# Two hybrid blocks on one core: the first block's gates, projection up and mixture laid out by channel, and the second attention's outputs turned ahead of the last fill

## The chip, the cores and the metric

The kernel runs on one core of a Trainium2 chip. The metric is the device time of one execution in microseconds (us); lower is better. The core has TensorE (PE; its weight loads are shown as PEld), VectorE (DVE), ScalarE (ACT), GpSimd (POOL) and the DMA queue engine SyncE (SP), each with an instruction queue of its own.

## The reference, cut to what matters

512 tokens of width 1024 pass through two blocks, all in float32. The first block mixes two attentions and then has a mixture of experts; the second has a recurrent branch and an attention of its own. The change touches the mixer of the first block only:

```
h = rms_norm(x, norm_mix_g)                       # 512 x 1024
(f_q, f_k, f_v, f_f, n_q, ..., g_a, g_b) = split_cols(h @ w_in)   # g_a, g_b: 1024 columns each
out_a = from_heads(fox_attention(...)) @ w_fox_up     # 512 x 512 @ 512 x 1024
out_b = from_heads(nsa_attention(...)) @ w_nsa_up     # 512 x 512 @ 512 x 1024
mix = sigmoid(g_a) * out_a + sigmoid(g_b) * out_b
x = x + mix @ w_out
x = x + hierarchical_moe(rms_norm(x, norm_ffn_g), ...)
```

The kernel takes a sigmoid as 0.5 * (1 + tanh(z / 2)), and leaves the factor 0.5 to the very end of the mixture.

## The kernel before, in words

**Products.** Float32 operands are kept as a high and a low half (`split`: ACT copies the high half, DVE subtracts), and each product is three matmuls (`mm3`). `linear_steps` makes a product of all tokens with some columns of a weight: tokens stand (128 at a time), weights move (256 or 512 columns), and the result lies with tokens on the partitions. It returns two lists of steps with a nominal cost each: loads (a DMA on SP, and the two halves of the weights by ACT and by DVE or POOL in turns, `weight_piece`), and products (one slice of 128 of the inner dimension each; the last one of a token tile calls `emit`, which empties the bank). Results go through the PSUM banks of tag "mm", of which there are two. A buffer is handed on when all who use it are done.

**Normalisation.** `hh` and `hl` are the halves of x * gain, turned (channels on partitions). The factor 1/rms of each token, `c.r`, with `c.rh` = `c.r` / 2, is applied when a bank is emptied; with tokens on the partitions it is a column of 128 scalars, and ACT takes it as the scale of its instruction.

**The mixer, `first_mixer`.** PE runs in the order in which the code is written (`manual_schedule`); on the other engines a planner orders the instructions by its own cost model. After a start-up, `A.run` goes through 24 attention jobs (8 heads of the first attention, 16 of the second) in 72 units: scores of one unit, transposes of the unit before, values of the one before that. Between them `fill.pull` takes steps from a long list (`Fill`) until their nominal costs reach the given time. The list holds, in this order, the input projections (q, k, v, kw, nq), small steps ("start"), the gates of the second attention (`gate`, four jobs of 256 channels, g0 to g512 and g), the turning of the first attention's outputs (`turn`), and four times 256 channels of the first attention's gate and projection up (`up`: a0, u0, ...). In `gate` ACT takes Tanh of the bank and SP stores it to `gd`. In `up` ACT takes Tanh (`gated`), and when the projection up of the same channels is done, DVE makes (1 + tanh) * product (`emit`), stored to `md` by ACT's queue. `gd` and `md` lie in DRAM with tokens as rows. `second` and `trig` prepare vectors for the second block; their tiles `small` and `cs` have the tag t, of which there are two buffers.

What is left of the list at the end of the attention run is done by `fill.until(None)`. Then `token_T` turns the second attention's outputs `ob` (four token tiles: four transposes on PE into an mm bank, a copy by ACT, four subtractions by DVE), and `merge` does the rest for each half of the channels: it loads `gd` and `md`, multiplies the outputs with `w_nsa_up` (512 columns moving), and per token tile DVE makes (1 + gate) * product and adds the other half of the mixture; four transposes on PE turn it, and ACT and DVE split it into `mh` and `ml`. These stand in the output projection, `out_proj` (in `route`), which begins right behind, token tile by token tile with eight products each. Then come the router and the experts, whose weights are streamed.

The lines that matter: `linear_steps` L128 to L148, `tanh_to_dram` L150, `token_T` L169, `merge` L181, `r_row` L248, `gate` L682, `turn` L688, `up` L694, the jobs L710 to L733, the run and what follows L771 to L782, `trig` L1921.

Of the kernel before, what the change touches and what calls it, by code (L numbers as in the profile page):

```python
# [10 lines left out]
FT = mybir.dt.float32  # L11
FR = mybir.dt.float32r
# [3 lines left out]
AF = mybir.ActivationFunctionType  # L16
OP = mybir.AluOpType
# [4 lines left out]
S = 512  # L22
D = 1024
NT = 4
# [16 lines left out]
class Ctx:  # L41
# [105 lines left out]
        return ([(max(1, g * n // 512), lambda k0=k0: load(k0)) for k0 in range(0, K, 128 * g)],  # L147
                [(3 * n / 2400, lambda i=i, k=k: product(i, k)) for i in range(NT) for k in range(K // 128)])  # L148

    def tanh_to_dram(self, pool, dst):  # L150

        def emit(i, ps):
            sg = pool.tile([128, 512], FT, name="sg", bufs=2)
            n = ps.shape[1]
            self.nc.scalar.activation(sg[:, :n], ps, AF.Tanh, scale=self.rh[:, i:i + 1])
            self.nc.sync.dma_start(dst(i), sg[:, :n])
        return emit

    def silu2_to_dram(self, pool, dst, scale=lambda i: 0.5):

# [84 lines left out]
        self.rh = self.sm.tile([128, NT], FT, name="rxh", bufs=1)  # L245
        nc.vector.tensor_scalar(self.rh, self.r, 0.5, None, op0=OP.mult)

    def r_row(self, t):  # L248

        n = t.shape[0]  # L250
        ps = self.bank("pt", [128, S])
        for i in range(NT):
            self.nc.tensor.matmul(ps[:n, 128 * i:128 * i + 128], self.r[:, i:i + 1].to_broadcast([128, n]), self.ident,
                                  start=True, stop=True)
        self.nc.scalar.activation(t, ps[:n], AF.Copy)
# [279 lines left out]
def first_mixer(c, I, at, hh, hl):  # L535

    nc, tc = c.nc, c.tc
    w_in = I["w_in"][0]
# [5 lines left out]
    def big(name, tag):  # L544
        return at.tile([128, NT, 512], FT, name=name, tag=tag, bufs=1)
# [13 lines left out]
    x = [big("x", t).rearrange("p (a i) n -> p a (i n)", a=2) for t in ("t0", "t1", "zk", "b2")]  # L559
    x, xgs, scr = [x[i // 2][:, i % 2] for i in range(4)], [x[3][:, i] for i in range(2)], x[2][:, 1]  # L560
# [11 lines left out]
    pt = c.bank("x", [128, S])  # L572
# [70 lines left out]
    N = Nsa(c, at)  # L643
# [12 lines left out]
    def fox(h):  # L656
        def scale():
            if h % 2 == 0:
                two["q"] = A.scaled(z["zq"][:, :, 64 * h:64 * h + 128].rearrange("p i (a d) -> p i a d", a=2),
                                    fx["q"][:, :, h:h + 2])  # L660
            two["k"] = A.twice(z["zk"][:, :, 64 * h:64 * h + 64], fx["k"][:, :, h:h + 1])

        def queries():
            if h % 2 == 0:
                qs[h:h + 2] = A.queries(two["q"], c.cv["fox_q"])

        def prep():
            k = A.keys(two["k"], c.cv["fox_k"])
            cb = at.tile([128, S], FT, name="cb", bufs=2)
            nc.sync.dma_start(cb, _ap(cumd, h * S, [[0, 128], [1, S]]))  # L670

            return A.passes(qs[h], k), lambda i: cb[:, :128 * (i + 1)], True

        def done(pv, rb, ri):

            nc.vector.scalar_tensor_tensor(z["zq"][:, :, 64 * h:64 * h + 64], pv, fx["v"][2], rb, op0=OP.mult, op1=OP.mult)
        return (scale, queries, prep), lambda: (*fx["v"][:2], h), done


    gd = c.dram.tile([S, D], FT, name="gd")  # L680

    def gate(c0):  # L682
        return c.linear_steps(hh, hl, w_in, 3872 + c0, 256, c.tanh_to_dram(at, lambda i: gd[
            128 * i:128 * i + 128, c0:c0 + 256]))
    md = c.dram.tile([S, D], FT, name="md")
    ot = []

    def turn(i):  # L688
# [4 lines left out]

    def up(c0):  # L694

        m = []

        def gated(i, ps):
            if i % 2 == 0:
                m.append(at.tile([128, 2, 256], FT, name="sg", bufs=2))  # L700
            nc.scalar.activation(m[i // 2][:, i % 2], ps, AF.Tanh, scale=c.rh[:, i:i + 1])

        def emit(i, ps):
            v = m[i // 2][:, i % 2]
            nc.vector.scalar_tensor_tensor(v, v, 1.0, ps, op0=OP.add, op1=OP.mult)
            nc.scalar.dma_start(md[128 * i:128 * i + 128, c0:c0 + 256], v)
        return {f"a{c0}": c.linear_steps(hh, hl, w_in, 2848 + c0, 256, gated),
                f"u{c0}": c.linear_steps(lambda: ot, None, I["w_fox_up"][0], c0, 256, emit)}

    jobs = {}  # L710
    for name, c0 in (("q", 0), ("k", 512), ("v", 1024)):
# [7 lines left out]
    def second():  # L719

        c.vectors([
            ("mu", I["mu_shift_2"], 0), ("w0", I["w0_2"], 0), ("a0", I["a0_2"], 0), ("k_k", I["k_k_2"], 0),
            ("k_a", I["k_a_2"], 0), ("r_k", I["r_k_2"].rearrange("a b -> (a b)"), 0), ("gn_gain", I["gn_gain_2"], 0),
            ("gn_bias", I["gn_bias_2"], 0), ("g_q", I["g_q_2"], 0), ("g_kv", I["g_kv_2"], 0),
        ], "mm")
        late.append(trig(c, I, at))
    jobs |= {f"g{c0}": gate(c0) for c0 in range(0, D - 256, 256)}
    jobs["second"] = ([], [(1.0, second)])
    jobs["g"] = gate(D - 256)
    jobs["trig"] = ([], [(0.5, lambda: late[0]())])  # L730
# [9 lines left out]
    pt = c.bank("pt", [128, NT, 32])  # L740
# [4 lines left out]
    f = at.tile([8, S], FT, name="t", bufs=2)  # L745
# [20 lines left out]
    with tc.manual_schedule(engines={mybir.EngineType.PE}):  # L766
        N.keys(I, A, z["kv"], fill)
        N.values(I, A, z["kv"], fill)
        fill.until("v")
        comp = [f for g in range(2) for f in N.compressed(g)]  # L770
        A.run([fox(h) for h in range(8)] + N.jobs(A, lambda: big("ob", "zk")), fill, lambda u: 2.0 if u <= 22 else 1.62,  # L771
              [(43 + 2 * n, f) for n, f in enumerate(comp)])
        fill.until(None)


    mix = [at.tile([128, 2, D], FT, name="mix", tag=t, bufs=1) for t in ("t0", "t1")]
    mh, ml = (c.hp.tile([128, 8, S], FR, name=n, tag="f16", bufs=2) for n in ("mh", "ml"))
    ot = at.tile([128, 4, S], FR, name="obh", tag="kv", bufs=1), [
        at.tile([128, S], FR, name="obl", tag=t, bufs=n) for t, n in (("p", 3), ("p", 3), ("p", 3), ("cb", 2))]
    c.token_T(N.ob, *ot)  # L780
    c.merge(at, "q", 8, lambda: ot, I["w_nsa_up"][0], gd, md, mix, mh, ml)
    return mh, ml  # L782


# [1136 lines left out]
def trig(c, I, pool):  # L1921

    nc = c.nc
    small = pool.tile([128, 8, NT, 16], FT, name="t", bufs=2)
    pi, pf, inv = small[:, 0, 0, :NT].bitcast(I32), small[:, 1, 0, :NT], small[:, 2, 0]
    nc.sync.dma_start(pi, I["positions_2"].rearrange("a (i p) -> p (a i)", p=128))
    nc.vector.tensor_copy(pf, pi)
    for j in range(16):  # L1930
        nc.gpsimd.memset(inv[:, j:j + 1], float(np.float32(10000.0) ** np.float32(-2.0 * j / 32)))
    sh = [128, NT, 16]
    ang, n = small[:, 3], small[:, 4]
    nc.vector.tensor_mul(ang, pf[:, :, None].to_broadcast(sh), inv[:, None, :].to_broadcast(sh))
    c1 = 6.28125
    c2 = math.floor((2 * math.pi - c1) * 2 ** 20) / 2 ** 20
    c3 = 2 * math.pi - c1 - c2
    cos, sin = small[:, 5], small[:, 6]
    for j, r in ((1, cos), (0, sin)):
        nc.vector.tensor_scalar(n, ang, 1.0 / (2 * math.pi), 0.25 * j, op0=OP.mult, op1=OP.add)  # L1940
        nc.vector.tensor_scalar(n, n, 12582912.0, None, op0=OP.add)
        nc.vector.tensor_scalar(n, n, -12582912.0, None, op0=OP.add)
        nc.vector.scalar_tensor_tensor(r, n, -c1, ang, op0=OP.mult, op1=OP.add)
        nc.vector.scalar_tensor_tensor(r, n, -c2, r, op0=OP.mult, op1=OP.add)
        nc.vector.scalar_tensor_tensor(r, n, -c3, r, op0=OP.mult, op1=OP.add)
        if j:
            nc.vector.tensor_scalar(r, r, math.pi / 2, None, op0=OP.add)
        nc.vector.tensor_scalar(r, r, 3.1415925, -3.1415925, op0=OP.min, op1=OP.max)
    nc.scalar.activation(small[:, 5:7], small[:, 5:7], AF.Sin)
    cs = pool.tile([128, NT, 128], FT, name="t", bufs=2)  # L1950
    nc.gpsimd.memset(cs, 0.0)
    nc.gpsimd.tensor_copy(cs[:, :, 64:80], cos)
    nc.gpsimd.tensor_copy(cs[:, :, 80:96], cos)
    nc.gpsimd.tensor_scalar(cs[:, :, 96:112], sin, -1.0, None, op0=OP.mult)
    nc.gpsimd.tensor_copy(cs[:, :, 112:], sin)
    c.csd = c.dram.tile([128, 2, NT, 16], FT, name="csd")
    nc.sync.dma_start(c.csd, small[:, 5:7])

    def turn():
        pt = c.bank("mm", [128, S])  # L1960
        for i in range(NT):
            nc.tensor.transpose(pt[:, 128 * i:128 * i + 128], cs[:, i], c.ident)
        qs = -1.0 / math.sqrt(96.0)
        csq = pool.tile([128, S], FT, name="sg", bufs=2)
        nc.gpsimd.memset(csq[:64], qs)
        nc.scalar.activation(csq[64:], pt[64:], AF.Copy, scale=qs)
        c.csqd = c.dram.tile([128, S], FT, name="csqd")
        nc.sync.dma_start(c.csqd, csq)
    return turn
# [317 lines left out]
```

## Time and profile before

| | us |
|---|---|
| median of 3 runs | 1434.35 |
| lowest, highest | 1432.84, 1443.26 |
| the profiled execution | 1437.92 |
| its span, first to last instruction | 1436.0 |

The profile is of one execution. Its page gives the busy time of each engine (matmuls are pipelined and their ends are modelled, so a busy PE is not PE at its peak); further views are the busy time by stretch, the list of who waited for whom, groups of instructions, and the timeline, whose times are counted from the first instruction. An L number is a line of the kernel before.

### The profile page before, as it was taken

The page shows a single profiled execution, that of the slowest core. Times are in us where ns is not written, and L with a number is a line of the kernel's source. Part 1 is how long each engine was busy: PE and PEld are TensorE (multiplying, and loading weights), DVE is VectorE, ACT ScalarE, POOL GpSimd, SP SyncE. Part 2 cuts the span into 40 slices and gives each one's busy share as a digit, 9 for nine tenths or more (in the row PEclk, how much of TensorE's full clock was granted, in tenths as well). Part 3 has the DMA queues.
Part 4 walks back from the last instruction along what each step waited for, and adds up shares of the span by engine and source line. Part 5 has one row for each costly group of instructions (what it writes and reads, how often), then busy time and mean ns, then how long its engine had stood idle before and what let it go on. Part 6 is the DMA issues. An engine that isn't in the chain of part 4 may idle for free.

```text
span 1436.0 us, 24621 instructions
## 1 busy us (share of the span) xinstructions
PE 1285.7 (90%) x9232; PEld 1090.5 (76%) x9232; DVE 951.4 (66%) x1907; ACT 753.9 (53%) x1291; POOL 427.3 (30%) x349
## 2 busy tenths in 40 slices
PE   7989777997989896899999997879988998799997
PEld 6889677987889775577777776868976767788875
DVE  5565557556565637799999997646657858525645
ACT  5544445665444322688888874645556664224431
POOL 1333324332332111235555522201123335213211
PEclk9999888999999998899999998989999999799999
DMA  6432222222133388999999986521152234233543
GB/s 195 119 106 76 63 54 61 86 64 66 60 96 115 98 285 328 320 356 364 355 345 359 343 292 209 148 83 48 46 165 74 83 123 123 87 100 115 169 135 118
DMA packets 162445, 230.94 MB, mean 161 GB/s; under 512 B 22426, under 2 KB 99021, under 8 KB 162320
## 3 DMA queue, kind: packets, MB, share of 16 engines
q1 hardware_dynamic: 150912, 205.44, 43.7%
q0 software_dynamic: 6224, 18.62, 4.6%
q10 hardware_dynamic: 5184, 5.25, 1.1%
q8 instruction: 74, 1.21, 0.3%
q14 instruction: 51, 0.42, 0.1%
HBM read 200.89 MB, written 30.36 MB: 161 GB/s over the span
## 4 chain that ended last, share of the span: by engine, by line
PE 37%; DVE 9%; DMA 5%; issue 5%; ACT 4%; POOL 1%; POOLq 0%; DVEq 0%; ACTq 0%; SPq 0%
PE mm L118 8%; PE mm L120 8%; PE mm L119 8%; DMA x2d<-y,slt 2%; PE s L120 2%; PE s L118 2%; PE s L119 2%; DMA raw<-in_w_in 2%; PE s L457 1%; DVE itmp L1766 1%; DVE Ti L1768 1%; DMA raw<-in_w_o 1%; PE pt L484 1%; DMA vmmx<-vmx 1%; POOL wl L112 1%
## 5 line engine op out<-in xcount | busy, mean ns | idle before, releaser
L112 POOL TENSOR_TENSOR wl<-raw,wh 128x512 fp32r<-128x512 f32 x119 | 163.7, 1381 | 462.9 <-ACT wh L109 424.2
L92 DVE TENSOR_TENSOR wl<-rawe,wh 128x1024 fp32r<-128x1024 f32 x192 | 224.8, 1218 | 23.9 <-ACT wh L90 22.9
L109 ACT ACTIVATE wh<-raw 128x512 fp32r<-128x512 f32 x214 | 131.6, 627 | 130.2 <-PE mm L120 57.6
L118 PE MATMUL mm<-wh,hh 128*128 128x256 f32 (+1 forms) x616 | 186.7, 303 | 11.1 <-ACT hh L90 3.5
L90 ACT ACTIVATE wh<-rawe 128x1024 fp32r<-128x1024 f32 x192 | 190.6, 1052 | 2.0 <-PE mm L120 1.8
L119 PE MATMUL mm<-wl,hh 128*128 128x256 f32 (+1 forms) x616 | 179.7, 292 | 0.3 <-DVE wl L112 0.3
L120 PE MATMUL mm<-wh,hl 128*128 128x256 f32 (+1 forms) x616 | 179.8, 292 | 0.1
L118 PEld LDWEIGHTS mm<-wh,hh 128*128 128x128 f32 (+1 forms) x616 | 122.8, 199 | 14.3 <-ACT hh L90 3.9
L1262 POOL DMA_INDIRECT xe<-td,slf x16 | 97.9, 6118 | 116.8 <-issue 73.4
L119 PEld LDWEIGHTS mm<-wl,hh 128*128 128x128 f32 (+1 forms) x616 | 122.6, 199 | 2.0 <-DVE wl L112 0.5
L120 PEld LDWEIGHTS mm<-wh,hl 128*128 128x128 f32 (+1 forms) x616 | 122.0, 198 | 0.9 <-DVE hl L92 0.4
L118 PE MATMUL mm<-wh,uh 128*128 128x256 f32 (+1 forms) x352 | 110.4, 314 | 12.9 <-DVE sg L2202 9.3
L112 DVE TENSOR_TENSOR wl<-raw,wh 128x512 fp32r<-128x512 f32 x95 | 79.4, 840 | 58.8 <-ACT wh L109 58.4
L475 ACT ACTIVATE p<-s,m 128x128 f32<-128x128 f32 (+3 forms) x128 | 67.3, 525 | 83.3 <-DVE m L471 62.6
L118 PE MATMUL mm<-wh,xh 128*96 128x512 f32 x256 | 103.8, 405 | 1.3 <-ACT xh L90 1.3
L119 PE MATMUL mm<-wl,uh 128*128 128x256 f32 (+1 forms) x352 | 104.7, 298 | 0.0
L120 PE MATMUL mm<-wh,ul 128*128 128x256 f32 (+1 forms) x352 | 104.5, 297 | 0.0
L120 PE MATMUL mm<-wh,xl 128*96 128x512 f32 x256 | 102.0, 398 | 0.4 <-DVE xl L92 0.4
L119 PE MATMUL mm<-wl,xh 128*96 128x512 f32 x256 | 101.2, 395 | 0.0
L488 DVE SCALAR_TENSOR_TENSOR pl<-pt,ph 128x384 f16<-128x384 f32 (+1 forms) x96 | 57.6, 600 | 39.1 <-ACT ph L487 38.5
L118 PEld LDWEIGHTS mm<-wh,uh 128*128 128x128 f32 x352 | 70.6, 200 | 15.6 <-DVE sg L2202 9.5
L119 PEld LDWEIGHTS mm<-wl,uh 128*128 128x128 f32 x352 | 70.7, 201 | 0.8
(717 smaller groups left out, 3390.0 us busy)
## 6 DMA issues: line engine op xcount, KB each, us to landing
raw<-in_w_in SPq DMA_DIRECT2D x71, 512.0 KB, 3.9
rawe<-in_w_gate SPq DMA_DIRECT2D x64, 512.0 KB, 10.7
rawe<-in_w_down SPq DMA_DIRECT2D x63, 512.0 KB, 11.5
rawe<-in_w_up SPq DMA_DIRECT2D x62, 512.0 KB, 12.1
gd<-sg SPq DMA_DIRECT2D x32, 128.0 KB, 1.9
g<-gd SPq DMA_DIRECT2D x16, 256.0 KB, 3.9
md<-sg ACTq DMA_DIRECT2D x32, 128.0 KB, 2.0
mix<-md SPq DMA_DIRECT2D x16, 256.0 KB, 3.8
```

The costliest lines, as they stand in the source:

```text
L90: nc.scalar.activation(hi, src, AF.Copy, scale=scale)
L92: nc.vector.tensor_sub(lo, src, hi.bitcast(FT))
L109: nc.scalar.activation(wh, raw[:, k:k + m], AF.Copy)
L112: e.tensor_sub(wl, raw[:, k:k + m], wh.bitcast(FT))
L118: nc.tensor.matmul(out, xh, wh, start=start, stop=False)
L119: nc.tensor.matmul(out, xh, wl, start=False, stop=False)
L120: nc.tensor.matmul(out, xl, wh, start=False, stop=stop)
L457: mm = nc.tensor.matmul(si, q[:, 128 * i:w], k[:, :w], start=a == 0, stop=a == len(passes) - 1)
L475: nc.scalar.activation(p[:, o:o + w], si, AF.Exp, bias=m, scale=-1.0)
L484: nc.tensor.transpose(pt[:, j:j + 128], p[:, j:j + 128], c.ident)
L488: nc.vector.scalar_tensor_tensor(pl[:, :w], pt[:, :w], PSC, ph[:, :w], op0=OP.mult, op1=OP.subtract)
L1262: nc.gpsimd.indirect_dma_start(out=xe, out_offset=None, in_=td, in_offset=bass.IndirectOffsetOnAxis(ap=of, axis=0))
```

## The change

The gates, the projection up and the merge make their products with weights standing: 128 channels at a time (`channel_steps`), all 512 tokens moving, so that the result lies with channels on the partitions. The factor 1/rms then runs along the free axis: a new fill step (`over`) spreads it over all partitions by four matmuls, and `opened` multiplies a bank by that row on DVE and takes Tanh on ACT. `gd` and `md` have channels as rows. `merge_channels` takes the place of `merge`: the mixture comes out turned, and its transposes are gone. `token_T` for `ob` moves from behind the remaining fill to ahead of it, with `obh` under another tag. `cs` in `trig` moves from tag t to tag sg.

```diff
-    def tanh_to_dram(self, pool, dst):
...
+    def channel_steps(self, xh, xl, w, c0, n, emit):
+
+        K = w.shape[0]
+        ws, bank = [], {}
+
+        def load(k0):
+            ws.extend(self.weight_piece(w[k0:k0 + 512, c0:c0 + n].rearrange("(k p) n -> p k n", p=128), [4, n]))
+
+        def product(a, k):
+            if k == 0:
+                bank[0] = self.bank("mm", [128, S])
+            h, l = (x[k] if isinstance(x, list) else x[:, k] for x in ((xh, xl) if xl is not None else xh()))
+            self.mm3(bank[0], *(x[:, 128 * a:128 * a + 128] for x in ws[k]), h, l, k == 0, k == K // 128 - 1)
+            if k == K // 128 - 1:
+                emit(c0 // 128 + a, bank[0])
+        return ([(max(1, 4 * n // 512), lambda k0=k0: load(k0)) for k0 in range(0, K, 512)],
+                [(0.64, lambda a=a, k=k: product(a, k)) for a in range(n // 128) for k in range(K // 128)])
+
+    def merge_channels(self, room, x, w, gd, md, mh, ml):
+
+        nc = self.nc
+        for c0 in range(0, D, 256):
+            g, m = {}, {}
+            for a in range(c0 // 128, c0 // 128 + 2):
+                g[a], m[a] = (room() for _ in range(2))
+                nc.sync.dma_start(g[a], gd[128 * a:128 * a + 128])
+                nc.sync.dma_start(m[a], md[128 * a:128 * a + 128])
+
+            def emit(a, ps, g=g, m=m):
+                nc.vector.scalar_tensor_tensor(g[a], g[a], 1.0, ps, op0=OP.add, op1=OP.mult)
+                nc.vector.tensor_add(m[a], m[a], g[a])
+                self.split(mh[:, a], ml[:, a], m[a], 0.5)
+            loads, products = self.channel_steps(*x, w, c0, 256, emit)
+            for _, f in loads + products:
+                f()
...
-    def r_row(self, t):
+    def r_row(self, t, bank="pt"):
...
-    gd = c.dram.tile([S, D], FT, name="gd")
+    gd = c.dram.tile([D, S], FT, name="gd")
+    row = []
+
+    def over():
+
+        row.append(at.tile([128, S], FT, name="t", bufs=2))
+        c.r_row(row[0], "mm")
+
+    def opened(ps):
+        sg = at.tile([128, S], FT, name="sg", bufs=2)
+        nc.vector.tensor_mul(sg, ps, row[0])
+        nc.scalar.activation(sg, sg, AF.Tanh, scale=0.5)
+        return sg
 
     def gate(c0):
-        return c.linear_steps(hh, hl, w_in, 3872 + c0, 256, c.tanh_to_dram(at, lambda i: gd[
-            128 * i:128 * i + 128, c0:c0 + 256]))
-    md = c.dram.tile([S, D], FT, name="md")
+        return c.channel_steps(hh, hl, w_in[:, 3872:], c0, 256, lambda a, ps: nc.sync.dma_start(
+            gd[128 * a:128 * a + 128], opened(ps)))
+    md = c.dram.tile([D, S], FT, name="md")
...
-        m = []
-
-        def gated(i, ps):
...
+        m = {}
+
+        def emit(a, ps):
+            nc.vector.scalar_tensor_tensor(m[a], m[a], 1.0, ps, op0=OP.add, op1=OP.mult)
+            nc.scalar.dma_start(md[128 * a:128 * a + 128], m[a])
+        return {f"a{c0}": c.channel_steps(hh, hl, w_in[:, 2848:], c0, 256, lambda a, ps: m.update({a: opened(ps)})),
+                f"u{c0}": c.channel_steps(lambda: ot, None, I["w_fox_up"][0], c0, 256, emit)}
...
+    jobs["row"] = ([], [(0.4, over)])
     jobs |= {f"g{c0}": gate(c0) for c0 in range(0, D - 256, 256)}
...
+        ot2 = at.tile([128, 4, S], FR, name="obh", tag="t0", bufs=1), [
+            at.tile([128, S], FR, name="obl", tag=t, bufs=n) for t, n in (("p", 3), ("p", 3), ("p", 3), ("cb", 2))]
+        c.token_T(N.ob, *ot2)
         fill.until(None)
 
-    mix = [at.tile([128, 2, D], FT, name="mix", tag=t, bufs=1) for t in ("t0", "t1")]
     mh, ml = (c.hp.tile([128, 8, S], FR, name=n, tag="f16", bufs=2) for n in ("mh", "ml"))
-    ot = at.tile([128, 4, S], FR, name="obh", tag="kv", bufs=1), [
-        at.tile([128, S], FR, name="obl", tag=t, bufs=n) for t, n in (("p", 3), ("p", 3), ("p", 3), ("cb", 2))]
-    c.token_T(N.ob, *ot)
-    c.merge(at, "q", 8, lambda: ot, I["w_nsa_up"][0], gd, md, mix, mh, ml)
+    c.merge_channels(lambda: at.tile([128, S], FT, name="mg", tag="q", bufs=8), ot2, I["w_nsa_up"][0], gd, md, mh, ml)
...
-    cs = pool.tile([128, NT, 128], FT, name="t", bufs=2)
+    cs = pool.tile([128, NT, 128], FT, name="sg", bufs=2)
```

## Rows read from the trace of the kernel before

**Rows 1.** Busy time on the page: us, share of the span, instructions.

```profile
PE 1285.7 (90%) x9232; PEld 1090.5 (76%) x9232; DVE 951.4 (66%) x1907; ACT 753.9 (53%) x1291; POOL 427.3 (30%) x349
```

**Rows 2.** Stretches: length, busy PE, PEld, DVE, ACT, POOL (count), granted clock, DMA share, GB/s.

```profile
235.00:455.00 220.00, 197.56 (x1956) 186.02 (x1955) 137.54 (x393) 116.92 (x231) 67.13 (x66) 1.00 0.25 77
455.00:471.46 16.46, 13.04 (x109) 12.04 (x108) 7.50 (x23) 6.91 (x12) 4.86 (x4) 0.91 0.56 166
471.46:500.86 29.40, 27.77 (x128) 22.49 (x129) 18.98 (x31) 8.40 (x14) 5.85 (x8) 0.94 0.20 65
474.00:475.00 1.00, 1.00 (x3) 0.72 (x3) 0.00 (x0) 0.00 (x0) 0.00 (x0) 0.50 0.00 0
475.00:476.00 1.00, 1.00 (x5) 0.85 (x4) 0.00 (x0) 0.00 (x0) 0.00 (x0) 0.89 0.00 0
```

**Rows 3.** PE's waits, 235 to 455 us: waiter, releaser, total us, times, longest.

```profile
PE mm L118 <- ACT sg L701: 2.4, 3, 1.1
PE pv L505 <- DVE tmp L976: 2.3, 3, 1.6
PE mm L118 <- ACT sg L155: 2.3, 2, 1.2
...
PE mm L118 <- DVE sg L705: 1.0, 2, 0.5
```

**Rows 4.** PE's timeline: start, duration, engine, line, operation, output and inputs, shape.

```profile
456.12 0.28 PE L120 MATMUL mm<-wh,hl 128*128 128x256 f32 x1
...
459.00 0.28 PE L120 MATMUL mm<-wh,hl 128*128 128x256 f32 x1
...
464.65 0.28 PE L120 MATMUL mm<-wh,oah 128*128 128x256 f32 x1
...
1074.40 0.39 PE L118 MATMUL mm<-uh,wh 128*128 128x512 f32 x1
...
1078.48 0.39 PE L118 MATMUL mm<-uh,wh 128*128 128x512 f32 x1
```

**Rows 5.** Instructions on tile sg: count, ns shortest, median, longest, first and last start.

```profile
L155 ACT ACTIVATE sg<-mm,rxh x16: 461/475/487, 239.5 to 321.7; 128x256 f32<-128x256 f32 x16
...
L705 DVE SCALAR_TENSOR_TENSOR sg<-sg,mm x16: 406/418/422, 363.1 to 465.0; 128x256 f32<-128x256 f32 x16
...
L164 ACT ACTIVATE sg<-zs x4: 629/633/634, 1194.7 to 1217.4; 128x512 f32<-128x512 f32 x4
```

**Rows 6.** Groups by shape, 464 to 508 us: busy us, mean ns, idle before, releaser.

```profile
L201 DVE SCALAR_TENSOR_TENSOR g<-g,mm 128x512 f32<-128x512 f32 x8 | 5.5, 685 | 7.0 <-PE mm L120 7.0
...
L1046 DVE TENSOR_TENSOR x<-mm,x 128x512 f32<-128x512 f32 x1 | 0.7, 692 | 3.0 <-DMA x<-in_x 3.0
```

**Rows 7.** Timelines of PE, DVE and POOL, 455 to 472 us; idle time before in brackets.

```profile
455.45 0.36 PE L118 MATMUL mm<-wh,hh 128*128 128x256 f32 x1
...
455.65 0.18 DVE L518 RECIPROCAL ri<-pv 128x4 f32<-128x4 f32 x1 [1.15 <-PE pv L507]
...
456.71 0.74 POOL L977 TENSOR_TENSOR ob<-ob,tmp 128x256 f32<-128x256 f32 x1 [4.91 <-DVE tmp L976]
...
464.80 1.30 PE L175 MATMUL mm<-ident,ob 128*128 128x128 f32 x8
468.67 1.94 PE L175 MATMUL mm<-ident,ob 128*128 128x128 f32 x8 [2.57 <-DVE obl L179]
471.46 0.77 PE L118 MATMUL mm<-wh,obh 128*128 128x512 f32 x1 [0.84 <-DVE obl L179]
```

**Rows 8.** Instructions of line 253: count, ns shortest, median, longest, first and last start.

```profile
L253 PE MATMUL pt<-ident,rx_y x16: 271/274/276, 49.4 to 908.8; 128*8 128x128 f32 x8, 128*128 128x128 f32 x8
```

**Rows 9.** PE's timeline around the output projection; idle time before in brackets.

```profile
500.48 0.63 PE L196 MATMUL pt<-ident,mix 128*128 128x128 f32 x4 [1.63 <-DVE mix L202]
...
513.89 0.29 PE L1137 MATMUL s<-wrs,th 128*128 128x40 f32 x1 [1.84 <-DVE wrs L92]
```

**Rows 10.** DMA issues on the page: count, KB each, median us to landing.

```profile
mix<-md SPq DMA_DIRECT2D x16, 256.0 KB, 3.8
```

More of the change, by code (lines that the diff above doesn't have):

```diff
@@ L148, in linear_steps @@
                 [(3 * n / 2400, lambda i=i, k=k: product(i, k)) for i in range(NT) for k in range(K // 128)])
-    def tanh_to_dram(self, pool, dst):
[L152 to L157, printed above, removed]
+    def channel_steps(self, xh, xl, w, c0, n, emit):
[27 more added lines that the diff above has]
+                f()
     def silu2_to_dram(self, pool, dst, scale=lambda i: 0.5):
@@ L246, in turned @@
         nc.vector.tensor_scalar(self.rh, self.r, 0.5, None, op0=OP.mult)
-    def r_row(self, t):
+    def r_row(self, t, bank="pt"):
         n = t.shape[0]
-        ps = self.bank("pt", [128, S])
+        ps = self.bank(bank, [128, S])
         for i in range(NT):
@@ L694, in up @@
     def up(c0):
-        m = []
-        def gated(i, ps):
[L699 to L708, printed above, removed]
+        m = {}
[4 more added lines that the diff above has]
+                f"u{c0}": c.channel_steps(lambda: ot, None, I["w_fox_up"][0], c0, 256, emit)}
     jobs = {}
```

## The prediction

> **What bounds the kernel now.** I read the page's busy times first: TensorE (PE) is busy for 90% of the span [rows 1]. That is an average over stages, so the next view is busy time by stretch, for the three stretches that the change touches [rows 2]. In the first (235 to 455 us, the two attentions with the fill between their steps) PE is busy for 197.56 of 220 us at a granted clock of 1.00, and VectorE (DVE) for 137.54. The order on PE is the order in which the kernel is written, so a late operand there is an idle PE. In the second (455 to 471.46, the rest of the fill and the turning of the second attention's outputs) PE is busy for 13.04 of 16.46 us, and in the third (471.46 to 500.86, the merge) for 27.77 of 29.40. Some of this is at the half clock (1.2 of 2.4 GHz): the granted clock was still 0.50 from 474 to 475 us and 0.89 in the next microsecond, after PE had idled 2.57 and 0.84 us between the transposes [rows 2, 7]. The list of who waited for whom then says what PE's idle time is in the first stretch: 5.7 us (2.4 + 2.3 + 1.0) are fill products that wait until ScalarE (ACT) or DVE has emptied one of the two mm banks; the largest wait for the softmax chain (tmp) is 2.3 us [rows 3]. So PE sets the pace in all three stretches, and a PE microsecond saved there should be a microsecond of the end. What follows, router and experts, waits for the output projection and shifts with it.
>
> **Part 1, pace of the fill.** Gates and projection up now have weights standing and 512 tokens moving, in half as many matmuls of twice the width. Uninterrupted, the 256-column products of the input projection run from 456.12 to 459.00 us in 24 steps, 0.120 us each; those of projection up end 48 steps later, at 464.65, 0.1177 us each. The same form as the new one exists in the second block: 18 steps from 1074.40 to 1078.48, 0.2267 us each [rows 4]. Fill matmuls before the change: 8 jobs of 32 products of 3, 768, and 4 jobs of 16 products of 3, 192. At the end of the attention run (455.45) 30 and 48 of them are left. So the attention run holds 738 x 0.120 + 144 x 0.1177 = 105.5 us of them. After the change there are 384 + 96 matmuls. The fill is pulled by nominal costs: what comes after job "v" adds up to 144.62, the run pulls 136.0 (3 x 3, 23 x 2, 49 x 1.62, 2 x 0.81), and 8.62 is left, which agrees with the 26 products of the trace. With the new row step (0.4) the sum is 145.02; in steps of 0.64 the run stops at 136.06, with 6 products of the last gated channel tile and 8 of projection up left, 42 matmuls. The run then holds 438 x 0.2267 = 99.3 us. **Saved: 6.2 us.**
>
> The Trainium skill ("TensorE: Matmul & The Clock Gate", section "Back-to-back issue gap") gives N/2.4 + 2.5 ns from one warm matmul to the next, 109 ns for 256 columns and 216 for 512. This case's rows don't agree, with 120 and 227, and the rows decide.
>
> **Part 2, banks.** An mm bank now takes 8 products of three, 5.4 us of fill instead of 2.9, until PE wants the other one again. The longest of the old bank waits is 1.2 us [rows 3], less than the added 2.5 us. All 5.7 us could go; since PE then comes earlier to the softmax chain, which is late next, I take 4.5. Bounds 0 and 5.7.
>
> **Part 3, what the emptying costs.** Before: 32 Tanh of 128x256 on ACT at 0.474 us, 15.2 us, with the scale in the same instruction [rows 5]. After: 16 multiplications from PSUM by the row on DVE, 0.69 us each as the 512-wide addition from PSUM [rows 6], 11.0 us, and 16 Tanh of 512, 0.633 us each, 10.1 us. The gating is 16 x 0.418 = 6.7 us before, and 8 x 0.685 = 5.5 after, by the merge's own instruction of that form [rows 5, 6]. DVE gains 9.8 us and ACT loses 5.1. DVE has 82 us idle in the stretch [rows 2], and the softmax has a whole unit of other PE work to run behind. But DVE runs in order and the maximum of each score tile is there too. Bounds: 0, and 9.8 if every added microsecond is handed on to PE; I take 2.0, near the lower end because the largest softmax wait is so small. Half as many and larger stores leave the SP queue (16 to 8 for the gates) and the ACT queue (16 to 8 for the products); no one waits for them, so nothing. The row itself is four matmuls of 0.274 us and one ACT copy, at most 1.1 us of PE [rows 8]; I take 0.8. The tile cs moves to the tag sg, so that the last two gate tiles share one buffer: the second waits for the first one's store and has 5.4 us for it; nothing.
>
> **Part 4, the outputs turned ahead of the last fill.** In the trace this costs PE from 464.80 to 471.46, 6.66 us [rows 7]. The order written now puts it right behind the last values, where the fill went on at 455.45, and two things come into the open that the remaining fill covers today. First, the result: DVE needs it from 455.65 on and POOL adds it into ob until 457.45, so PE waits 2.1 us. Second, the banks: the fill is stopped in the middle of an accumulation (6 products to go), which holds one of the two mm banks, and the four tiles must pass through the other one by one. A round is four transposes, the ACT copy, four DVE subtractions and the release: in the trace the transposes from 468.67 and the first merge matmul, which waits for their bank until 471.46, are 2.8 us apart at the half clock; at the full one it is 2.4, as eight transposes take 1.30 us instead of 1.94 [rows 7] and the copy starts earlier. So 2.1 + 2.4 + 2 x 2.8 + 1.0 for the last four = 11.1 us, from 455.45 to 466.55. The DVE work of the last tile is hidden by the fill. Then 42 matmuls, 9.5 us, and 1.8 us for starting them at the half clock, half of the 3.6 us that it lasted from 471.46 on. The merge would begin at 477.85, against 471.46: **6.4 us lost.** Bounds of the 11.1: 8.0 if two banks were free, as in the trace (3.87 from 464.80 to 468.67, 1.94, and the wait), and 15 if a weight copy on ACT and DVE (0.63 and 0.69 by the rows of that width) comes between in each of three rounds.
>
> **Part 5, the merge.** Before, from 471.46 to 500.86, it is 29.4 us [rows 2]: 96 matmuls of 512 columns, the first at the half clock, eight groups of four transposes between them, and at the end 1.63 us of waiting for the last mixture [rows 9]. After: 96 x 0.2267 = 21.8 us and no transposes. The last channel tile's four steps, three on DVE and one on ACT of 0.69 us at most [rows 6], take 2.8 us, and the output projection needs it only as the eighth of its first products, 4.8 us in: hidden. **Saved: 7.6 us.** The 16 loads of gates and mixture are the same in size. Eight go into the buffers of the queries, free by then; the other eight follow when the first channel tiles are done, on SP's queue, behind weight loads that wait for free buffers. The next tile is some 10 us away then, and a load landed in 3.8 us (median) [rows 10], so nothing; at worst 4 us. Router rows and x are loaded behind the merge's weights, and PE waited 1.84 us at 513.89 for the router's weights [rows 9]. Where their buffers will come free I can't see: 3 us either way, taken as 0.
>
> **Sum:** -6.2 - 4.5 + 2.0 + 0.8 + 6.4 - 7.6 = -9.1 us. The profiled execution took 1437.92 us with a span of 1436.0, and so would take 1428.8; it lies 3.6 us above the median of the runs, 1434.35, from which the forecast is 1425.3.
>
> **Rivals.**
> *The attention keeps its own pace* (0.22). Softmax waits grow by what the fill saves, as the cover per half unit shrinks and comes in lumps of 0.68 us instead of 0.36. For it: part 3. Against it: PE's 90% in the stretch and its small softmax waits. Parts 1 and 2 fall away: +1.6, 1436; half of it, 1431.
> *Softmax behind the gate's scaling* (0.12, slower). Each of the 16 multiplications (0.69) and its Tanh (0.633) stands in DVE's and ACT's order ahead of a score tile's maximum and exponential, and PE waits for p. Without the gain from banks and the 2.0 of part 3 the rest of the sum is -6.6; 16 x 1.32 = 21.1 us in full make it +14.5, 1449. It decides the sign once five of the 16 are handed on whole (6.6). Against it: today's 32 Tanh stand in ACT's order too and cost 4.7 us of bank waits.
> *More than forecast* (0.12). The bank chain runs at its lower bound (-3), all bank waits go (-1.2), DVE's extra work costs nothing (-2), and x and router weights come early (-3): 1416.
> *Only columns count* (0.06). If between attention steps two narrow matmuls took no longer than a wide one, part 1 would be nothing: 1431. Against it: 2 x 0.120 against 0.2267 us [rows 4], uninterrupted though. The Trainium skill's gap, named in part 1, is near this: 2.5 ns for each of the 444 matmuls that go from the run, 1.1 us, 1430.
> The forecast itself, 1420 to 1431, has 0.48.
>
> **Range and chances.** 1415 to 1440 takes in the forecast, the first and the last rival, nearly all of the third and a third of the slower one. About 1% (14.3 us) is what a measurement of this kernel can tell from no change; below 1420 lies the third rival and a tail of the forecast, 0.16; above 1448.7 the end of the slower one, 0.04; within 1%, 0.80.
>
> **What would show it.** Fill matmuls 0.227 us apart with wh as the standing operand; no wait for an mm bank in the attention run; the last values of the second attention some 8 us earlier than 455.45; then a PE wait of 2 us for ob, and four groups of four transposes 2.3 to 2.8 us apart, at a clock of 0.50, rather than two groups of eight; a merge of 22 us without idle time, and the output projection right behind it. The forecast is wrong if the last values come at the old time, if the transposes come in pairs, or if merge products wait for g or mg.

## The result: 1426.49 us, and the profile after

The changed kernel takes 1426.49 us (median of 8 runs, 1425.79 to 1432.65) beside 1435.61 us for the kernel before in the same comparison (8 runs, 1432.84 to 1443.26). The ratio is 0.9941, 95% interval 0.9916 to 0.9965: 0.6% faster, 5 to 12 us. The profiled execution took 1428.67 us with a span of 1426.8, against 1437.92 and 1436.0 before. That is 9.2 us less, where the sum of the forecast's terms was 9.1. The agreement is closer than the terms deserve: those for the banks and the emptying were wrong and nearly cancelled, and what the width of the matmuls saves came about otherwise than forecast. The experiments show which.

The page's busy times of the changed kernel; they answer to [rows 1]. PE has 504 matmuls less, but only 4.8 us less busy time: in the fill there are half as many, twice as wide.

```profile
PE 1280.9 (90%) x8728; PEld 1055.4 (74%) x8728; DVE 959.2 (67%) x1915; ACT 752.1 (53%) x1276; POOL 426.5 (30%) x349
```

Stretches of the changed kernel (columns as in [rows 2]): the two attentions with their fill, then the turning and the rest of the fill, then the merge.

```profile
235.00:447.80 212.80, 194.08 (x1518) 152.60 (x1516) 142.93 (x396) 113.87 (x217) 66.89 (x67) 0.99 0.24 74
447.80:470.43 22.63, 15.04 (x64) 11.79 (x61) 7.97 (x23) 5.76 (x10) 3.98 (x4) 0.77 0.17 58
470.43:492.40 21.97, 21.97 (x97) 18.03 (x96) 17.36 (x25) 9.08 (x15) 5.15 (x5) 1.00 0.69 204
```

In the merge PE is busy all the time at a granted clock of 1.00; before, [rows 2], it was 29.40 us with 27.77 busy. The stretch ahead of it is the price: 15.04 us busy of 22.63, at a mean clock of 0.77. Its timeline (start, duration, engine, line, operation; idle time before in brackets) answers to [rows 7]:

```profile
447.77 0.20 PE L535 MATMUL pv<-sh,pl 128*128 128x65 f16 x1
447.80 0.52 PE L203 MATMUL mm<-ident,ob 128*128 128x128 f32 x3
450.82 0.33 PE L203 MATMUL mm<-ident,ob 128*128 128x128 f32 x1 [2.50 <-POOL ob L1011]
452.85 1.09 PE L203 MATMUL mm<-ident,ob 128*128 128x128 f32 x4 [1.70 <-DVE obl L207]
455.63 1.08 PE L203 MATMUL mm<-ident,ob 128*128 128x128 f32 x4 [1.70 <-DVE obl L207]
458.41 1.08 PE L203 MATMUL mm<-ident,ob 128*128 128x128 f32 x4 [1.70 <-DVE obl L207]
459.15 0.78 PE L118 MATMUL mm<-hh,wh 128*128 128x512 f32 x1
...
470.43 0.39 PE L118 MATMUL mm<-obh,wh 128*128 128x512 f32 x1
...
492.41 0.40 PE L118 MATMUL mm<-wh,mh 128*128 128x512 f32 x1
...
505.88 0.29 PE L1171 MATMUL s<-wrs,th 128*128 128x40 f32 x1 [2.18 <-DVE wrs L92]
```

The last values (447.77) come 7.7 us earlier than in the trace before. PE then waits for ob, and the four tiles go one by one through the one free mm bank, 2.78 us apart. The fill goes on at 459.15, slowly at first (0.78 us for a matmul that takes 0.39 at the full clock). The merge takes 21.98 us and the output projection starts right behind it. The wait for the router's weights grew from 1.84 us [rows 9] to 2.18.

The waits of PE in the changed attention run, 233 to 447.78 us (columns as in [rows 3]):

```profile
PE pv L533 <- DVE tmp L1010: 1.9, 2, 1.0
PE mm L118 <- DVE sg L718: 1.7, 2, 1.2
...
PE mm L118 <- DVE sg L739: 0.7, 2, 0.3
PE mm L1996 <- DVE sg L718: 0.5, 1, 0.5
```

The waits for an mm bank that the emptying of gates and products holds are 2.9 us (1.7 + 0.7 + 0.5), where [rows 3] had 5.7 (5.9 with one of 0.2 that they leave out).

Two stretches serve as yardsticks below. **The run** goes from the softmax's 18th exponential (counted from 0; 233 us in, ahead of the first gate) to the last values. **The tail** goes from the last values to the output projection. The run was 221.36 us before and 214.74 after, the tail 45.44 and 44.64. These are the rows of the run, first of before, then of after:

```profile
234.06:455.42 221.36, 198.92 (x1977) 187.03 (x1975) 138.48 (x400) 117.49 (x232) 67.22 (x67) 0.99 0.25 76
```

```profile
233.03:447.77 214.74, 196.02 (x1527) 154.19 (x1527) 144.90 (x408) 114.41 (x219) 66.89 (x67) 0.99 0.24 74
```

PE's busy time fell by 2.9 us and its idle time by 3.7 (22.44 to 18.72), although DVE has 6.4 us more to do. Of the rest of the 9.2, 0.8 is in the tail. The other 1.8 us are 1.0 ahead of the run, where nothing was changed, and 0.8 behind the start of the output projection (935.1 to 934.4 us). Both are within what these two stretches differ by among all the profiles below: 227.1 to 236.8 us ahead of the run, 933.8 to 941.4 from the output projection to the end.

### The profile page after: what moved, and what is told of

Read it like the earlier page. It is cut to its first block, busy times and chain, and to the rows that moved or that the text cites. A ratio compares the mean times of both kernels' runs of the same rounds, so it can differ in the third digit from the quotient of the medians.

```text
span 1426.8 us, 23593 instructions
## 1 busy us (share of the span) xinstructions
PE 1280.9 (90%) x8728; PEld 1055.4 (74%) x8728; DVE 959.2 (67%) x1915; ACT 752.1 (53%) x1276; POOL 426.5 (30%) x349
## 4 chain that ended last, share of the span: by engine, by line
PE 41%; DVE 10%; DMA 6%; issue 5%; ACT 4%; POOL 1%; SPq 0%; DVEq 0%; POOLq 0%; ACTq 0%
PE mm L118 9%; PE mm L120 9%; PE mm L119 9%; DMA raw<-in_w_in 2%; DMA x2d<-y,slt 2%; PE s L120 2%; PE s L118 2%; PE s L119 2%; PE s L485 1%; DVE itmp L1800 1%; DVE Ti L1802 1%; POOL wl L112 1%; ACT wh L109 1%; PE pt L512 1%; DMA vmmx<-vmx 1%
## 5 line engine op out<-in xcount | busy, mean ns | idle before, releaser
L118 PE MATMUL mm<-wh,hh 128*128 128x256 f32 (+1 forms) x360 | 109.8, 305 | 6.2 <-ACT hh L90 3.6
L119 PE MATMUL mm<-wl,hh 128*128 128x256 f32 (+1 forms) x360 | 107.3, 298 | 0.3 <-DVE wl L112 0.3
L120 PE MATMUL mm<-wh,hl 128*128 128x256 f32 (+1 forms) x360 | 107.4, 298 | 0.1
L118 PEld LDWEIGHTS mm<-wh,hh 128*128 128x128 f32 (+1 forms) x360 | 73.6, 204 | 7.5 <-ACT hh L90 4.0
L119 PEld LDWEIGHTS mm<-wl,hh 128*128 128x128 f32 (+1 forms) x360 | 73.6, 205 | 1.2 <-DVE wl L112 0.5
L120 PEld LDWEIGHTS mm<-wh,hl 128*128 128x128 f32 (+1 forms) x360 | 73.2, 203 | 1.0 <-DVE hl L92 0.4
```

What stands on the lines that cost most here:

```text
L118: nc.tensor.matmul(out, xh, wh, start=start, stop=False)
L119: nc.tensor.matmul(out, xh, wl, start=False, stop=False)
L120: nc.tensor.matmul(out, xl, wh, start=False, stop=stop)
```

## Experiments

All ratios are to the kernel before, measured on the same chip.

### Where the outputs are turned

**e1_turn_behind** puts the turning back behind the last fill:

```diff
-        c.token_T(N.ob, *ot2)
         fill.until(None)
+        c.token_T(N.ob, *ot2)
```

> The changed kernel with the turning of the second attention's outputs put back behind the remaining fill. My theory (the move costs time: 11.35 us of PE from the last values to the end of the transposes in the changed kernel, because the result is awaited in the open and one mm bank is held by the half-done accumulation): here the transposes cost PE about what they cost in the kernel before, 6.7 us from their start to the first merge matmul, in pairs of tiles, so the output projection begins 4 to 5 us earlier than in the changed kernel and the median is about 1422. Rival (the move pays, because ACT's and DVE's part of the turning is hidden by the fill): 4 to 7 us slower than the changed kernel, about 1432.

**e2_four_banks** leaves it where the change put it, but lets the tiles pass through the two s and the two pt banks, which are free by then:

```diff
-            pt = self.bank("mm", [128, 4, 128])
+            pt = self.bank("mm" if tiles else ("s", "pt")[i % 2], [128, 4, 128])
```

> The changed kernel, the turning ahead of the fill, but through four PSUM banks (two of tag s, two of tag pt, idle by then) instead of the one mm bank that is left. My theory (three waits of 1.70 us for that bank): these three waits go, the wait of 2.5 us for ob stays, PE is not idle long enough to lose much at the half clock: 5 to 7 us less than the changed kernel, about 1421. Rival (ACT and DVE set the pace of the turning, not the bank): the waits move to the next matmul that needs the turned tiles or a bank, and less than 2 us is gained.

**e3_turn_in_fill** does that too, and pulls a part of the fill first:

```diff
+        fill.until("a768")
         c.token_T(N.ob, *ot2)
         fill.until(None)
```

> As the four-bank version, and the turning stands after the remaining six products of the last gated channel tile, so that 4 us of fill cover the wait for ob. My theory: neither the bank waits (5.1 us) nor the wait for ob (2.5 us) is left, and PE never falls to the half clock (1.8 us): 9 to 10 us less than the changed kernel, about 1417. Rival (as for the four banks: ACT and DVE set the pace): not more than 3 us less.

Measured: e1 1427.61 us (1423.17 to 1432.48), ratio 0.9934 [0.9910, 0.9958], tail 38.20 us. e2 1425.05 us (1421.68 to 1428.58), 0.9927 [0.9903, 0.9951], tail 37.72. e3 **1418.25 us** (1415.93 to 1422.96), 0.9875 [0.9851, 0.9900], tail 33.45. The changed kernel's tail is 44.64.

PE's timeline of e1: the transposes come behind the fill, at the full clock, and cost 4.82 us (460.55 to 465.37). The merge then begins slowly: the granted clock is 0.53 in the 3.63 us from 465.37 on.

```profile
460.55 0.60 PE L203 MATMUL mm<-ident,ob 128*128 128x128 f32 x4
461.56 0.66 PE L203 MATMUL mm<-ident,ob 128*128 128x128 f32 x4 [0.41 <-DVE sg L739]
463.05 0.63 PE L203 MATMUL mm<-ident,ob 128*128 128x128 f32 x4 [0.83 <-DVE obl L207]
463.91 0.63 PE L203 MATMUL mm<-ident,ob 128*128 128x128 f32 x4 [0.24 <-DVE obl L207]
465.37 0.66 PE L118 MATMUL mm<-obh,wh 128*128 128x512 f32 x1 [0.83 <-DVE obl L207]
```

PE's timeline of e2: of the waits only the one for ob is left.

```profile
446.72 0.52 PE L203 MATMUL s<-ident,ob 128*128 128x128 f32 x3
449.74 0.33 PE L203 MATMUL s<-ident,ob 128*128 128x128 f32 x1 [2.50 <-POOL ob L1011]
449.90 0.60 PE L203 MATMUL pt<-ident,ob 128*128 128x128 f32 x4
450.34 0.60 PE L203 MATMUL s<-ident,ob 128*128 128x128 f32 x4
450.78 0.81 PE L203 MATMUL pt<-ident,ob 128*128 128x128 f32 x4
462.43 0.39 PE L118 MATMUL mm<-obh,wh 128*128 128x512 f32 x1
```

Stretches of e3, the run and the tail: in the tail PE has no idle time at all, and the clock stays at 1.00.

```profile
236.82:451.50 214.68, 196.67 (x1530) 154.52 (x1528) 144.50 (x403) 114.42 (x219) 66.75 (x67) 0.99 0.24 74
451.50:484.95 33.45, 33.45 (x161) 27.73 (x158) 25.10 (x48) 14.34 (x25) 9.57 (x8) 1.00 0.56 173
```

So the place of the turning, as the change has it, costs 11.2 us of the tail beside the best one tried: 6.9 of them go with the banks, the other 4.3 with the wait for ob (2.5) and the slower matmuls behind it (the mean clock of e2's tail is 0.95, of e3's 1.00). With both gone the interval lies wholly below the changed kernel's, and e3 is the fastest version here. The three kernels' runs took 215.2, 214.5 and 214.7 us, so up to there they are the changed kernel again.

The median of e1 was no lower than the changed kernel's, in spite of the 6.4 us. That called for both on one chip, unchanged: **e7_after_again** and **e8_behind_again** (the edit of e1).

> The changed kernel once more, on the chip on which the next kernel runs, as its yardstick: 1426.5 us, 44.6 us from the last values to the output projection, 214.7 from the 18th exponential to the last values.

> e1_turn_behind once more (the outputs turned behind the last fill), beside the changed kernel on one chip. Its first run saved 6.4 us between the last values and the output projection, but its median was no lower than the changed kernel's, which ran on another chip. Theory: the 6.4 us are real and what followed was chance (the clock behind the wait for the router's weights was 0.72 instead of 0.86 in that run): the median is 4 to 7 us below that of e7_after_again, about 1421. Rival: something behind the output projection gives the gain back in this order (a load that now comes too late, a wait that grows): the stretch is again 6 us shorter, the time within 2 us of e7_after_again, and the stretch from the output projection to the first expert's gather is again 82 us instead of 79.

Measured: e7 1429.47 us (12 runs, 1424.83 to 1434.88), ratio 0.9958 [0.9939, 0.9978], tail 44.31 us; e8 1425.79 us (7 runs, 1419.26 to 1429.12), 0.9930 [0.9901, 0.9958], tail 36.63. The tail is 7.7 us shorter; it is 1.6 us shorter than that of e1 because the clock stayed at 1.00 behind the transposes. The median is 3.7 us lower than that of e7, just below the 4 to 7 of the theory, and the two intervals overlap. From the output projection to the arrival of the first expert's gathered rows e8 took 78.8 us, not 82, so that part of the rival is refuted. But from there to the end it lost 4 to 5 us again (860.1 us, e7 855.5), as e1 did (859.0, the changed kernel 855.3). The stretches from the output projection to the end, of the changed kernel, e7, e1 and e8 in this order:

```profile
492.40:1426.80 934.40, 853.34 (x5531) 687.43 (x5529) 654.09 (x1153) 512.51 (x824) 277.17 (x173) 0.95 0.60 199
```

```profile
496.00:1430.80 934.80, 850.40 (x5531) 683.48 (x5529) 654.37 (x1153) 512.09 (x824) 276.60 (x173) 0.95 0.61 199
```

```profile
489.00:1430.00 941.00, 854.59 (x5531) 687.91 (x5529) 653.29 (x1153) 512.33 (x824) 277.33 (x173) 0.94 0.60 198
```

```profile
485.20:1424.00 938.80, 853.92 (x5531) 687.37 (x5529) 655.67 (x1153) 512.01 (x824) 276.20 (x173) 0.94 0.60 198
```

The work is the same and the mean clock a hundredth lower, but that alone doesn't say why: e3 took 935.9 us there, also at 0.94. e4 (below), in the order of the changed kernel, took 941.0 us as well, so it can be chance; that the order of e1 and e8 brings it about isn't excluded, and stays open.

### What the width of the fill's matmuls is worth

**e5_narrow** makes each wide fill matmul as two, in the same bank; **e6_halves** gives each half a bank of its own:

```diff
+            for k in range(k0, k0 + S // width):
...
-            self.mm3(bank[0], *(x[:, 128 * a:128 * a + 128] for x in ws[k]), h, l, k == 0, k == K // 128 - 1)
+                self.mm3(bank[0][:, t:t + width], *(x[:, 128 * a:128 * a + 128] for x in ws[k]),
+                         h[:, t:t + width], l[:, t:t + width], k == 0, k == K // 128 - 1)
```

> The changed kernel with each wide fill matmul of gates and projection up made as two of 256 tokens (first all of the left half of a bank, then all of the right one). Layout, emptying, bank cadence and the merge's wide matmuls stay as they are. It tells the term for the pace of the fill alone. As forecast (0.120 against 0.2267 us): 438 wide ones become 876 narrow ones, +6.0 us in the attention run and +0.6 behind it, about 1433 us. As the traces of before and after now read (127 ns a narrow, 249 ns a wide one, waits taken out): 876 x 0.127 - 108.5 = +2.8 us in the run, +0.5 behind it, about 1430. Only columns count: 0, about 1426.5. In the profile: from the 18th exponential of the softmax to the last values 214.7 us in the changed kernel; 220.7, 217.5 or 214.7 here. Waits for an mm bank stay at 2.4 to 2.9 us.

> As e5_narrow (256 tokens a matmul, by channel), but each half is a bank of its own, emptied by itself (32 multiplications and 32 Tanh of 256 columns, stores whole): PE wants the other mm bank after 24 narrow matmuls, as in the kernel before, instead of 48. It tells the bank term alone, by its difference to e5_narrow. Theory (half as many bank changes removed about 3 of the 5.7 us of bank waits): waits for mm banks 5 to 6 us in the run, the stretch from the 18th exponential to the last values some 3 us longer than in e5_narrow (220.5), the time about 1433 us. As forecast (4.5 us): 222, about 1434.5. Rival (the bank waits only changed their name, since PE meets the softmax chain instead): the stretch as in e5_narrow, 217.5, about 1430, with other waits smaller by as much.

Measured: e5 1433.68 us (12 runs, 1430.54 to 1439.02), ratio 1.0007 [0.9989, 1.0026]; e6 1431.07 us (12 runs, 1427.77 to 1439.46), 0.9996 [0.9975, 1.0018]. Both have lost what the change had won. The run of e5, then that of e6:

```profile
232.48:452.60 220.12, 199.23 (x1967) 187.07 (x1965) 146.82 (x403) 113.17 (x218) 68.22 (x67) 0.99 0.23 72
```

```profile
227.11:447.47 220.36, 201.28 (x1965) 189.53 (x1965) 147.78 (x429) 114.95 (x233) 67.21 (x67) 0.98 0.24 72
```

Undoing the width costs 5.4 us of the run (220.12 - 214.74), near the 6.0 that the forecast gives. The medians agree in kind: the interval of e5 lies above both of the changed kernel's, by ratio they are 0.5 to 0.7% apart, and e5 and e7, on one chip, are 4.2 us apart as they stand.

But little of it is where the forecast had it. The mean distance from one fill matmul to the next start, waits taken out, is 0.2487 us for the 438 wide ones of the changed kernel's run and 0.1257 for the 876 narrow ones of e5: 108.9 and 110.1 us in all. Two narrow matmuls cost 2.6 ns more than a wide one, 1.2 us for all pairs. PE's busy time rises by 3.2 us, so the other matmuls of the run take part in it, which no kernel here explains; the 2.8 us expected from the two traces was near this. Its idle time rises by 2.2, which a price per matmul doesn't hold. The added waits are spread over several kinds and not the same in all four kernels with narrow matmuls. The largest rise in e5 is in the wait of the transposes for the softmax's exponential; here it is in the changed kernel, then in e5:

```profile
PE pt L512 <- ACT p L503: 0.9, 1, 0.9
```

```profile
PE pt L515 <- ACT p L506: 2.6, 3, 1.3
```

e6 refutes the two expectations by which the cadence counts. With the old cadence the run isn't 3 us or more longer than e5's but 0.2, although PE was at the half clock for 10.2 us of it (4.0 in e5), and no bank waits come back. PE's waits in e6's run:

```profile
PE mm L118 <- DVE sg L722: 0.9, 3, 0.5
...
PE mm L118 <- DVE sg L747: 0.6, 1, 0.6
...
PE mm L2005 <- DVE sg L722: 0.3, 1, 0.3
```

### What emptying on DVE costs, and whether it removed the waits

**e4_no_row** lets the Tanh empty the bank and leaves the multiplication out, in the changed kernel; **e9_halves_tanh** is the same edit in e6, and **e10_halves_again** is e6 beside it:

```diff
-        nc.vector.tensor_mul(sg, ps, row[0])
-        nc.scalar.activation(sg, sg, AF.Tanh, scale=0.5)
+        nc.scalar.activation(sg, ps, AF.Tanh, scale=0.5)
```

> The changed kernel without the multiplication by the row: ACT takes Tanh straight from the bank (it leaves out the factor 1/rms in both gates). It takes 11 us of DVE work out of the attention run. My theory (DVE has room, the multiplication is handed on to PE in small part): 1 to 3 us less than the changed kernel. Rival (the multiplications stand ahead of the softmax in DVE's order and PE waits for it): 6 to 11 us less.

> e6_halves with the bank emptied by the Tanh itself on ACT, as in the kernel before, and no multiplication on DVE (the factor 1/rms of both gates is left out): bank cadence and emptying are then those of before, by channel. In e6_halves the old cadence brought no bank waits back (1.8 us), so theory: what had made them was the emptying on ACT, whose Tanh stands in order behind the softmax's exponentials, and not the cadence. Then waits for mm banks (released by ACT, sg) are 4 to 6 us here, twice those of the next kernel and more. Rival: neither, the old waits belonged to the old layout's places in the order: 2 us here too. Cadence, as forecast: it would have shown in e6_halves already.

> e6_halves once more, as yardstick on the same chip: 1.8 us of waits for mm banks released by DVE (sg); 220 us from the 18th exponential to the last values, less if the clock falls less often than in its first run.

Measured: e4 1433.75 us (12 runs, 1426.48 to 1435.96), ratio 0.9966 [0.9947, 0.9985], run 215.81 us; single executions of e9, 1427.96 us, run 218.83, and of e10, 1434.22 us, run 219.73. Taking away 8.4 us of DVE's busy time (144.90 to 136.50 in the run of e4) brought nothing that can be told from noise: the run is 1.1 us longer in the one pair, at a mean clock of 0.98 instead of 0.99, and 0.9 shorter in the other, at 1.00 instead of 0.98. In the profiles the longer time of e4 lies behind the start of the output projection (941.0 against 934.4 us), as said. The bank waits of e9's run:

```profile
PE mm L118 <- ACT sg L722: 1.4, 3, 0.7
...
PE mm L118 <- DVE sg L746: 0.6, 1, 0.6
PE mm L2004 <- ACT sg L722: 0.4, 1, 0.4
```

These are 2.4 us, not 4 to 6: with the old cadence and the old engine at the bank the waits of [rows 3] still don't return. What is left is that gates and products were laid out by token before, and with it where among the attention's steps a bank changes; no kernel here isolates it.

## Why the prediction was right, and which terms were not

The time was forecast at 1425.3 us and is 1426.49; the likeliest case happened. By its steps:

- **Part 1, pace of the fill, 6.2 us.** The size came out, the mechanism only in part. Undone by e5 it is 5.4 us of the run, but between before and after PE's busy time in the run fell by 2.9, and between e5 and after the fill's own matmuls make 1.2. The price of 0.2267 us was taken from uninterrupted products; in the run the three matmuls of a gate's product pay 0.268, 0.233 and 0.245 (mean distance to the next start, waits taken out). The premise of the rival "only columns count" nearly holds for these distances, with 2.6 ns for two narrow matmuls in place of a wide one instead of the forecast's 13; its time of 1431 us doesn't, as the width also changes waits and other matmuls. By the isolated gap of the Trainium skill ("TensorE: Matmul & The Clock Gate", section "Back-to-back issue gap") it would be 2.5 ns; the run agrees with that difference, though not with the two gaps themselves (126 and 249 ns here).
- **Part 2, banks, 4.5 us.** The failed step: "An mm bank now takes 8 products of three, 5.4 us of fill instead of 2.9". The bank waits did fall, from 5.7 to 2.9 us, but not for this reason: e6 has the old cadence, 1.8 us of such waits and the run of e5. The other 1.2 us of the run (221.36 to the 220.12 of e5) are all that layout, cadence, emptying and the row step bring together in this pair of profiles. The reading was also narrower than the list: PE's two largest waits in it, which neither [rows 3] nor the prediction has, are for banks of the attention, and the first is still 3.7 us after the change.

```profile
PE x L118 <- DVE tmp L1032: 3.7, 4, 1.8
PE x L349 <- DVE q L362: 3.5, 2, 2.4
```

- **Part 3, emptying and row, 2.0 + 0.8 us.** The 2.0 was too dear as far as single profiles can tell: e4, and e9 beside e10, show no clear gain when the multiplications go. With 82 idle us in [rows 2] DVE had room for them. No kernel isolates the 0.8 of the row. The rival "softmax behind the gate's scaling" is refuted, as the wait of pv for tmp, 2.3 us in [rows 3], is now 1.9. Parts 2 and 3 together were forecast at -1.7 us, and e5 shows -1.2: two wrong terms that cancelled, by luck. The rival "the attention keeps its own pace" fails too, with a run that is 6.6 us shorter.
- **Part 4, outputs turned, 6.4 us lost.** Right. Wait for ob 2.5 us (2.1 forecast), rounds 2.78 (2.8; the first 2.03, not 2.4), 11.35 us to the fill's return (11.1), then 11.28 for the rest of it (11.3). The merge started 22.66 us behind the last values, 6.62 us more than before. e2 confirms the banks, e3 both causes.
- **Part 5, merge, 7.6 us.** Right: 21.98 us against 29.40, 7.4 less, without idle time. The loads of gates and mixture and the last channel tile stayed hidden.
- **Taken as nothing:** the wait for the router's weights, 0.3 us longer.

The tail as a whole gained 0.8 us, where parts 4 and 5 said 1.2. What the measured -6.6 and -0.8 leave of the 9.2 is 1.8 us in code that the change doesn't touch, and it ran the favourable way. That the time came within 1.2 us of the forecast is therefore partly luck: e7, the same kernel, was 5.3 us below the kernel before in its median where the first comparison had 9.1.

## What to carry to other kernels

Price a wide matmul against two narrow ones from an experiment that changes the width alone, and look where its time goes: here the run got 5.4 us longer, but two narrow matmuls took only 2.6 ns more than a wide one, 1.2 us in all, where uninterrupted products promised 13 ns. The rest lay in waits and in other matmuls. A list of waits names who came last, not what would be gained: change the cadence in a run of its own before a bank wait is entered as a gain. And ahead of a step that waits for a result of another engine, leave a few microseconds of independent work and pass it through banks that are idle: e3 won as much again as the whole change with two lines.

## What the runs showed of the hardware

**The same program, nearly the same waits, another clock.** e7 is the changed kernel once more; its run took 218.86 us instead of 214.74. Rows of the changed kernel's first profile, then of e7, around the same place:

```profile
322.00:324.00 2.00, 0.98 (x7) 0.74 (x7) 1.62 (x7) 1.19 (x4) 0.73 (x1) 1.00 0.88 324
324.00:326.00 2.00, 1.44 (x17) 1.25 (x17) 1.02 (x4) 1.00 (x2) 0.00 (x0) 1.00 0.00 0
326.00:328.00 2.00, 1.17 (x18) 1.19 (x18) 1.44 (x8) 0.88 (x3) 0.00 (x0) 1.00 0.00 0
...
233.00:448.00 215.00, 196.28 (x1529) 154.44 (x1529) 144.93 (x409) 114.67 (x219) 66.89 (x67) 0.99 0.24 73
```

```profile
323.00:325.00 2.00, 0.93 (x15) 0.95 (x15) 1.35 (x5) 1.23 (x4) 0.00 (x0) 1.00 0.24 89
325.00:327.00 2.00, 1.12 (x7) 0.94 (x7) 1.15 (x6) 0.70 (x2) 0.00 (x0) 0.70 0.00 0
327.00:329.00 2.00, 2.00 (x17) 1.93 (x16) 1.34 (x6) 1.16 (x3) 0.00 (x0) 0.50 0.00 0
329.00:331.00 2.00, 2.00 (x10) 1.88 (x10) 1.27 (x4) 0.88 (x3) 0.00 (x0) 0.50 0.00 0
331.00:333.00 2.00, 1.80 (x8) 1.27 (x6) 1.70 (x6) 1.72 (x5) 1.04 (x1) 0.59 0.00 0
...
233.00:452.00 219.00, 202.63 (x1530) 159.66 (x1530) 144.83 (x404) 114.73 (x218) 66.75 (x67) 0.96 0.22 72
```

In both PE is idle for about half of the 4 us of the first two rows (1.58 and 1.95 us). In the one the granted clock stays at 1.00 (2.4 GHz); in the other it falls to 0.50 (1.2 GHz) for some 7 us. Why it fell in the one and not in the other isn't shown. The last row of each fence is the whole run: mean clock 0.99 and 0.96, so e7 spent about 13 us more at the half clock ((0.04 x 219 - 0.01 x 215) x 2; with rows of 1 us added up, 17.9 against 3.4 us) and lost 4.1. A difference of that size between two single profiles of a run need not be the effect of an edit. The verdict on width rests on more than that: with narrow matmuls e5, e6 and e10 took 220.1, 220.4 and 219.7 us at mean clocks of 0.98 to 0.99, and e9 218.8 at 1.00; with wide ones four profiles at 0.98 to 0.99 (the changed kernel, e1, e2, e3) took 214.5 to 215.2. PE of e5 and of the changed kernel was at the half clock for about as long, 4.0 and 3.4 us. Only e7 and e8, at 0.96, come near the narrow ones (218.9 and 218.8).
